# Attention's softmax divisors: turned by VectorE in 32x32 blocks and sent round through DRAM, instead of turned by TensorE

## The chip, the cores and the metric

One core of a Trainium2 chip runs one program. The metric is the time of one execution on the device, in microseconds (us). The kernel before took 1761.09 us (median of 3 runs, 1760.48 to 1762.41).

Engines are named as the profile names them: PE is TensorE (PEld its weight loads), DVE is VectorE, ACT is ScalarE, POOL is GpSimd, SP is SyncE, which here only issues DMAs. Each engine runs its own instructions strictly in the order in which they stand in the program; engines wait for each other through semaphores.

## The reference, cut to what matters

Layer 0 is windowed grouped-query attention with a sink logit per head; layer 1 is a Mamba-2 mixer, which the change does not touch. For every block of 128 queries:

```
s = einsum('bqkgd,bskd->bkgqs', qb, kb).astype(float32) * scale      # 16 heads, 4 KV heads, head dim 64
p = softmax(concatenate([where(mask, s, -inf), sink_col], -1), -1)[..., :-1]
o = einsum('bkgqs,bskd->bqkgd', p, vb)
y_lat = (o * silu(g)) @ w_out
```

The softmax's divisor is one number for each query and head. The kernel does not divide `p`; it multiplies the gate `silu(g)` by the reciprocal of the sum, and then `o` by that. There are 1024 latent queries (8 blocks, each seeing up to 3 latent blocks and 2 context blocks of keys) and 256 context queries (2 blocks that see only the context).

## The kernel before, in words

The program runs, in order: adaLN and the q, k, v, g projections (up to some 250 us), the attention with the other projections woven in (some 250 to 685 us), the tail of the output projection, and layer 1 (from some 700 us). Only the attention has lines that the change touches.

The attention is cut into 40 **units**, one for each block `b` of 128 queries and each KV head `j` with its `R = 4` query heads: first 8 units of the two context blocks (2 key blocks each), then 32 of the latent blocks 0 to 7 (4 or 5 key blocks each). A unit has two halves:

- `att_front`: PE makes the scores `S` (queries on the partitions) for each head; DVE (L781) masks them and takes the row minimum `nm`, ACT (L783) takes the exponential into `sm` and adds up `sums`. POOL adds the sink's term (L786, L788), DVE takes the reciprocal of the 128x4 `sums` (L790).
- `att_back`: for each key block, PE turns the four heads' `sm` (L802) into one of the two `pt` buffers in PSUM, ACT copies it to `ph` (L806), DVE makes the low part `pl` (L807), and PE multiplies both by `v` into `pv` (L808, L809). `pv` has one buffer and holds the head dimension on the partitions and the queries along the row. At the unit's end ACT copies half of `pv` to `co` (L818), DVE adds the halves into `ot` (L821), POOL multiplies by the gate `sgt` (L822), and ACT and POOL split the product for the output projection (L824, L825).

The gate `sgt` also has the head dimension on the partitions, so the 128x4 reciprocals, which have queries on the partitions, must be turned and repeated over each head's 64 partitions. Before the change, POOL widens them to 128x256 (`rs`, L791, one buffer), PE turns the two halves through `pt` (L815, two transposes a unit), and DVE multiplies `sgt` by the result in PSUM (L816).

`att_front` of the next unit is written ahead of `att_back` of this one. What stands in each engine's row is settled by a scheduler when the program is built: each engine gets the ready instructions by priority, and the projections for later (L240 to L242, with their weights loaded by SP at L233, cast by ACT at L223, split by POOL at L225) are put between. `issue_after(x)` adds an ordering edge behind `x`, without a semaphore, to instructions of `x`'s own engine.

Of the kernel before, what the change touches and what calls it, by code (L numbers as in the profile page):

```python
# [9 lines left out]
F32 = mybir.dt.float32  # L10
# [7 lines left out]
P = 128  # L18
# [11 lines left out]
HD = 64  # L30
# [3 lines left out]
R = 4  # L34
# [8 lines left out]
    pj=1, S=2, pt=2, pv=1,  # L43
    rope_b=2, qf=3, qh=3, ql=2, kHH=2, kLL=2, qs=2, sgt=2, sm=8, mx=2, nm=2, es=2, sums=2, ph=2, pl=2, co=1, ot=2,
    oraw=3, h1=3, h1k=8, wada=6, gq=1, sqa=1,
    cacc=2, cctx=1, bT=2, cT=2, xn4=4, xn2=1, bn4=4, bn2=1, sz=2, xw=2, hf=2, hx=2, M=2, bw=2, y2=1, xs=1, uT=2, pj2=2, psX=3, sk=2, dg=2,
)
G0 = 4
AHEAD = 1
# [65 lines left out]
class Kernel:  # L115
# [13 lines left out]
    def t(self, pool, shape, dt, tag, bufs=None):  # L129
        self.n += 1  # L130
        kw = {"bufs": bufs or BUFS.get(tag, 1)}
        return pool.tile(shape, dt, tag=tag, name=f"{tag}_{self.n}", **kw)
# [616 lines left out]
    def att_front(self, p, x, i, j, b):  # L749
        nc, t = self.nc, self.t  # L750
        ps = self.psA
        o = b * P - TT[i][0]
        sg = t(self.psm, [P, 2, P], F32, "sgt")
        nm = t(p, [P, R], F32, "nm")
        sums = t(p, [P, R], F32, "sums")
        qs = t(p, [P, R, P], F32R, "qs")
        nc.gpsimd.dma_start(qs, self.q_d[j][i][:, :, :, o : o + P].rearrange("e s d n -> (s d) e n"))
        nc.sync.dma_start(sg, self.sg_d[j][i][:, :, o : o + P].rearrange("e p n -> p e n"))

        z = j % 2  # L760
        qz = self.qz[z]
        nc.gpsimd.dma_start(qz[z * HD : (z + 1) * HD], self.q_d[j][i][:, z, :, o : o + P].rearrange("e d n -> d e n"))
        if b < 8:
            k0, k1 = max(b - 1, 0), min(b + 2, 8)
        else:
            k0, k1 = 8, 8
        kb = list(range(k0, k1)) + [8, 9]
        c0_ = 512 - (k1 - k0) * P
        m0 = {0: 128, 7: 640}.get(b, 0 if b < 8 else 384)
        W = len(kb) * P  # L770
        sms = []
        for r in range(R):
            S = t(self.psS, [P, 1024], F32, "S")
            for x, (qq, kk) in enumerate(((qs[:, r, :], self.kHH[j]), (qz[:, r, :], self.kL[j // 2]))):
                if k1 > k0:
                    nc.tensor.matmul(S[:, c0_:512], qq, kk[:, k0 * P : k1 * P], start=x == 0, stop=x == 1)  # L776
                scored = nc.tensor.matmul(S[:, 512:768], qq, kk[:, LAT : LAT + CTX], start=x == 0, stop=x == 1)  # L777
            self.scored.append(scored.ins)
            Sv = S[:, c0_:768]
            sm = t(self.psm, [P, 640], F32, "sm")  # L780
            nc.vector.tensor_tensor_reduce(out=sm[:, :W], in0=Sv, in1=self.mask[:, m0 : m0 + W], scale=-SCALE, scalar=self.nsink[:, 4 * j + r : 4 * j + r + 1],  # L781
                                           op0=ALU.add, op1=ALU.min, accum_out=nm[:, r : r + 1])
            nc.scalar.activation(sm[:, :W], sm[:, :W], AF.Exp, bias=nm[:, r : r + 1], scale=-1.0, accum_out=sums[:, r : r + 1])  # L783
            sms.append(sm)
        es = t(p, [P, R], F32, "es")
        nc.gpsimd.tensor_tensor(es, nm, self.sink[:, 4 * j : 4 * j + 4], op=ALU.add)  # L786
        nc.scalar.activation(es, es, AF.Exp)
        nc.gpsimd.tensor_tensor(sums, sums, es, op=ALU.add)  # L788
        rs = t(self.pb, [P, 2, 2, HD], F32, "rs")
        nc.vector.reciprocal(sums, sums)  # L790
        nc.gpsimd.tensor_copy(rs, sums.rearrange("p (x e) -> p e x", e=2).unsqueeze(3).broadcast_to([P, 2, 2, HD]))  # L791
        return j, b, i, o, kb, sms, sg, rs

    def att_back(self, p, st, oH, oL, tick):
        nc, t = self.nc, self.t
        ps = self.psA
        j, b, i, o, kb, sms, sg, rs = st
        pv = t(ps, [P, 512], F32, "pv")
        for x, bb in enumerate(kb):
            pt = t(ps, [P, R, P], F32, "pt")  # L800
            for r in range(R):
                nc.tensor.transpose(pt[:, r, :], sms[r][:, x * P : (x + 1) * P], self.ident)  # L802
            ph = t(self.pb, [P, R * P], F32R, "ph")
            pl = t(self.pb, [P, R * P], F32R, "pl")
            ptf = pt.rearrange("p r n -> p (r n)")
            nc.scalar.copy(ph, ptf)  # L806
            nc.vector.tensor_sub(pl, ptf, ph)  # L807
            nc.tensor.matmul(pv, self.v[:, bb, j, :], ph, start=x == 0, stop=False)  # L808
            mm = nc.tensor.matmul(pv, self.v[:, bb, j, :], pl, start=False, stop=x == len(kb) - 1)  # L809
            self.last.append(mm.ins)  # L810
            tick()

        pt = t(ps, [P, 512], F32, "pt")
        for e in range(2):
            nc.tensor.transpose(pt[:, e * P : (e + 1) * P], rs[:, e].rearrange("p x d -> p (x d)"), self.ident)  # L815
        nc.vector.tensor_mul(sg, sg, pt[:, : 2 * P].rearrange("p (a n) -> p a n", a=2))  # L816
        co = t(self.pb, [HD, 512], F32, "co")
        nc.scalar.copy(co, pv[HD:, :])  # L818
        ot = t(self.pb, [P, 2, P], F32, "ot")
        for e in range(2):  # L820
            nc.vector.tensor_add(ot[e * HD : (e + 1) * HD].rearrange("p a n -> p (a n)"), pv[:HD, e * 256 : (e + 1) * 256], co[:, e * 256 : (e + 1) * 256])  # L821
        nc.gpsimd.tensor_tensor(ot, ot, sg, op=ALU.mult)  # L822
        oh = oH[i][:, 2 * j : 2 * j + 2, o : o + P]
        nc.scalar.copy(oh, ot)  # L824
        nc.gpsimd.tensor_tensor(oL[i][:, 2 * j : 2 * j + 2, o : o + P], ot, oh, op=ALU.subtract)  # L825

    def attention(self, c0, ckv):
        nc, t, a = self.nc, self.t, self.a
        ps = self.psA
# [4 lines left out]
        p = self.pool("att", ctx=c0)  # L834
# [3 lines left out]
        self.load_rope(pq, 512, 512)  # L838
        oH, oL = [None] * 3, [None] * 3
        self.qz = [t(p, [P, R, P], F32R, f"qz{z}") for z in range(2)]  # L840
        for z in range(2):
            nc.gpsimd.memset(self.qz[z][(1 - z) * HD : (2 - z) * HD].bitcast(F32), 0.0)

# [102 lines left out]
        for x, (i, j, b) in enumerate(units):  # L946
            if oH[i] is None:
# [6 lines left out]
                n = TT[i][1]  # L954
# [12 lines left out]
        with ExitStack() as c1:  # L967
# [6 lines left out]
            for i, lo in ((2, 256), (0, 0)):  # L974
                n = TT[i][1] // 2
# [889 lines left out]
```

## Time and profile before

| | |
|---|---|
| runs | 1761.09 us median (1760.48 to 1762.41, 3 runs) |
| profiled execution | 1762.06 us, of which the profiled span is 1760.4 us |
| granted TensorE clock | 0.997 |
| busy, share of the span | PE 98%, PEld 85%, DVE 68%, ACT 50%, POOL 44% |
| the chain that ended last | PE 89%, DVE 4%, ACT 2%, DMA 2%, issue 2% |

The span goes from the first to the last instruction. Busy time of PE counts matmuls that overlap in its pipeline, so 98% does not say that nothing could be squeezed; the chain of work that ended last says which engine set the pace. Idle time of an engine off that chain costs nothing by itself.

### The profile page before, as it was taken

How to read it: one execution, taken by the hardware profiler on the slowest of the kernel's cores; microseconds unless marked ns; L12 is line 12 of the kernel's file. 1: busy time of each engine (PE TensorE's matmuls, PEld its weight loads, DVE VectorE, ACT ScalarE, POOL GpSimd, SP SyncE). 2: the span in 40 equal slices, each digit the busy share in tenths (PEclk: the TensorE clock that was granted, in tenths of full speed). 3: DMA queues.
4: the chain of work that ended last, by engine and by line, in shares of the span. 5: the costliest groups of instructions: out<-in, count | busy, mean ns of one | idle time of the engine just before them, and what ended most of it. 6: DMA issues, size and time to landing. Idle time of an engine off the chain costs nothing.

```text
span 1760.4 us, 28922 instructions
## 1 busy us (share of the span) xinstructions
PE 1732.0 (98%) x10277; PEld 1498.0 (85%) x10277; DVE 1197.1 (68%) x2131; ACT 873.3 (50%) x1905; POOL 771.8 (44%) x1048
## 2 busy tenths in 40 slices
PE   9999999999999999999999999999999999999997
PEld 6897878888888787889898998989889898988886
DVE  5744436788877777585767867677686767776734
ACT  4522247777777775462544534344444444544522
POOL 3331046555565541004454544636455363554311
PEclk9999999999999999999999999999999999999999
DMA  9468866444564436222233332332333333655533
GB/s 362 172 197 259 288 178 144 102 114 96 115 163 129 120 101 226 69 70 66 79 83 90 75 91 69 88 78 76 90 82 80 85 82 78 181 168 172 176 96 132
DMA packets 211389, 225.53 MB, mean 128 GB/s; under 512 B 15788, under 2 KB 149036, under 8 KB 211244
## 3 DMA queue, kind: packets, MB, share of 16 engines
q1 hardware_dynamic: 177180, 205.02, 39.0%
q0 software_dynamic: 34064, 18.65, 5.9%
q8 instruction: 81, 1.33, 0.3%
q14 instruction: 64, 0.52, 0.1%
HBM read 188.78 MB, written 35.13 MB: 127 GB/s over the span
## 4 chain that ended last, share of the span: by engine, by line
PE 89%; DVE 4%; ACT 2%; DMA 2%; issue 2%; POOL 0%; SPq 0%; DVEq 0%; ACTq 0%; POOLq 0%
PE pj L1243 20%; PE pj L1277 10%; PE pj L1682 7%; PE pj L240 7%; PE pj L241 6%; PE pj L242 6%; PE psD L1227 4%; PE pt L802 3%; PE psX L1430 3%; PE psD L1346 2%; PE pv L809 2%; PE pv L808 2%; PE S L776 2%; PE S L777 2%; PE psX L1399 2%
## 5 line engine op out<-in xcount | busy, mean ns | idle before, releaser
L240 PE MATMUL pj<-uH,wh 128*128 128x512 f32 (+1 forms) x632 | 234.0, 370 | 4.2 <-ACT uH L824 1.5
L242 PE MATMUL pj<-uH,wl 128*128 128x512 f32 (+1 forms) x632 | 222.2, 352 | 0.0
L241 PE MATMUL pj<-uL,wh 128*128 128x512 f32 (+1 forms) x632 | 222.1, 351 | 0.0
L1321 POOL TENSOR_TENSOR xw<-xn,dtdec 128x256 f32<-128x256 f32 x144 | 96.0, 668 | 212.6 <-PE psD L1346 72.3
L1243 PE MATMUL pj<-uH,wh 128*128 128x512 f32 x512 | 173.2, 410 | 0.0
L1243 PE MATMUL pj<-uH,wl 128*128 128x512 f32 x512 | 170.3, 403 | 0.0
L1243 PE MATMUL pj<-uL,wh 128*128 128x512 f32 x512 | 168.7, 403 | 0.0
L1277 PE MATMUL pj<-wl,uH 128*128 128x256 f32 x512 | 150.8, 295 | 0.0
L1277 PE MATMUL pj<-wh,uH 128*128 128x256 f32 x512 | 150.3, 293 | 0.0
L1277 PE MATMUL pj<-wh,uL 128*128 128x256 f32 x512 | 149.8, 293 | 0.0
L807 DVE TENSOR_TENSOR pl<-pt,ph 128x512 fp32r<-128x512 f32 x168 | 115.0, 688 | 46.0 <-ACT ph L806 44.8
L240 PEld LDWEIGHTS pj<-uH,wh 128*128 128x128 f32 x632 | 119.6, 189 | 22.9 <-issue 3.6
L242 PEld LDWEIGHTS pj<-uH,wl 128*128 128x128 f32 x632 | 119.4, 189 | 18.4 <-DVE wl L225 1.3
L781 DVE CUSTOM_DVE_ANT_0 sm<-S,mask,nsink 128x640 f32<-128x640 f32 (+2 forms) x160 | 118.9, 773 | 23.8 <-PE S L777 18.2
L1462 ACT ACTIVATE uT<-psX,nw 128x128 f32<-128x128 f32 x128 | 46.6, 364 | 170.9 <-PE psX L1461 169.9
L225 POOL TENSOR_TENSOR wl<-wr,wh 128x512 fp32r<-128x512 f32 x74 | 97.2, 1317 | 77.5 <-ACT wh L223 74.0
L241 PEld LDWEIGHTS pj<-uL,wh 128*128 128x128 f32 x632 | 120.0, 190 | 12.0 <-issue 0.8
L783 ACT ACTIVATE sm<-sm,nm 128x640 f32<-128x640 f32 (+2 forms) x160 | 118.6, 743 | 21.2 <-DVE nm L781 20.6
L806 ACT CAST ph<-pt 128x512 fp32r<-128x512 f32 x168 | 97.9, 585 | 50.5 <-PE pt L802 47.6
L223 ACT CAST wh<-wr 128x512 fp32r<-128x512 f32 (+1 forms) x116 | 74.7, 648 | 83.4 <-PE pj L241 60.3
L1243 PEld LDWEIGHTS pj<-uH,wl 128*128 128x128 f32 x512 | 95.8, 188 | 19.9
L1243 PEld LDWEIGHTS pj<-uL,wh 128*128 128x128 f32 x512 | 95.3, 188 | 19.2
(357 smaller groups left out, 4913.0 us busy)
## 6 DMA issues: line engine op xcount, KB each, us to landing
wr<-w_x SPq DMA_DIRECT2D x32, 512.0 KB, 4.4
M<-acs SPq DMA_DIRECT2D x64, 256.0 KB, 5.1
bw<-acs SPq DMA_DIRECT2D x64, 256.0 KB, 5.4
wr<-w_sk SPq DMA_DIRECT2D x24, 512.0 KB, 4.5
wr<-wg SPq DMA_DIRECT2D x40, 256.0 KB, 4.8
qs<-q POOLq DMA_DIRECT2D x40, 256.0 KB, 4.0
wada<-w_ada SPq DMA_DIRECT2D x16, 512.0 KB, 8.3
wr<-wq SPq DMA_DIRECT2D x32, 256.0 KB, 3.2
```

The lines of the kernel that those rows point to most:

```text
L225: (eng or nc.vector).tensor_tensor(l, raw, h, op=ALU.subtract)
L240: self.nc.tensor.matmul(ps, lh, rh, start=first and i == 0, stop=False)
L241: self.nc.tensor.matmul(ps, lh, rl, start=False, stop=False)
L242: self.last_mm = self.nc.tensor.matmul(ps, ll, rh, start=False, stop=last and i == n - 1)
L781: nc.vector.tensor_tensor_reduce(out=sm[:, :W], in0=Sv, in1=self.mask[:, m0 : m0 + W], scale=-SCALE, scalar=self.nsink[:, 4 * j + r : 4 * ...
L783: nc.scalar.activation(sm[:, :W], sm[:, :W], AF.Exp, bias=nm[:, r : r + 1], scale=-1.0, accum_out=sums[:, r : r + 1])
L806: nc.scalar.copy(ph, ptf)
L807: nc.vector.tensor_sub(pl, ptf, ph)
L1243: self.pe = nc.tensor.matmul(raw[:, 512 * i : 512 * i + 512], l[:, k, :], r[i][:, k, :], start=k + y == 0, stop=k == KT - 1 and y == 2)
L1277: self.pe = nc.tensor.matmul(pj[:, c], l, r[:, k, :], start=c % 2 + q + k + y == 0, stop=c % 2 == 1 and q == 1 and k == 3 and y == 2)
L1321: nc.gpsimd.tensor_tensor(xw, X(st, c).rearrange("p (r h) -> p r h", r=R), self.dtdec[:, c, hd(d, g)].unsqueeze(2).broadcast_to([P, R, HP] ...
L1682: self.pe = nc.tensor.matmul(banks[x], l[:, z, sl], r, start=k == 2 * qs[0] and y == 0, stop=k == 2 * qs[-1] + 1 and y == 2)
```

## The change

The widening copy on POOL, the two transposes on PE and the multiplication out of PSUM go. In their place DVE takes the reciprocals in the first 4 columns of a 128x32 buffer (`s32`, two of them, zeroed once at the start) and turns that buffer in four 32x32 blocks into `sT`. SP stores it to DRAM as 32 short rows of 128 numbers (rows 0 to 3 are the four heads), and two DMAs of SP load it back, each spreading two heads' rows over 64 partitions (`rb`, tag `rs`, two buffers). DVE then multiplies `sgt` by `rb`, both in SBUF.

```diff
-        sums = t(p, [P, R], F32, "sums")
+        s32 = self.s32.pop(0)
+        self.s32.append(s32)
+        sums = s32[:, :R]
...
-        rs = t(self.pb, [P, 2, 2, HD], F32, "rs")
         nc.vector.reciprocal(sums, sums)
-        nc.gpsimd.tensor_copy(rs, sums.rearrange("p (x e) -> p e x", e=2).unsqueeze(3).broadcast_to([P, 2, 2, HD]))
+        turned = t(p, [P, 32], F32, "sT", 2)
+        nc.vector.transpose(turned, s32)
+        rs = t(self.dr, [32, P], F32, f"rs{j}_{b}")
+        nc.sync.dma_start(rs.rearrange("r (b n) -> b r n", b=4), turned)
...
         pv = t(ps, [P, 512], F32, "pv")
+        rb = t(self.pb, [P, 2, P], F32, "rs")
+        def spread():
+            for x in range(2):
+                nc.sync.dma_start(rb[x * HD : (x + 1) * HD], rs[2 * x : 2 * x + 2].unsqueeze(0).broadcast_to([HD, 2, P]))
+        if len(kb) < 4:
+            spread()
...
+            if x == 1 and len(kb) >= 4:
+                with self.tc.issue_after(mm.ins):
+                    spread()
...
-        pt = t(ps, [P, 512], F32, "pt")
-        for e in range(2):
-            nc.tensor.transpose(pt[:, e * P : (e + 1) * P], rs[:, e].rearrange("p x d -> p (x d)"), self.ident)
-        nc.vector.tensor_mul(sg, sg, pt[:, : 2 * P].rearrange("p (a n) -> p a n", a=2))
+        nc.vector.tensor_mul(sg, sg, rb)
```

The change moves the schedule of the whole attention. Three lines of the kernel get new numbers: the multiplication of the gate L816 becomes L828, the sum into `ot` L821 becomes L833, and the low part L807 becomes L819; the mask line L781 becomes L783; the store is L795, the loads back L807.

Two places show what moved. The first is DVE, in the latent blocks 0 to 3. Before, this piece holds the end of a unit: the gate's product (`sgt_1053`) stands seven instructions ahead of the same unit's `ot` (`ot_1129`), and the unit's reciprocal stands 28 rows ahead of the product.

```order
L781 ISA nm_1131_4832 128x1
L807 TENSOR_TENSOR pl_1126_4811<-pt_1124_4805,ph_1125_4810 128x512
L816 TENSOR_TENSOR sgt_1053_4540<-sgt_1053_4540,pt_1127_4819 128x256
L630 TENSOR_TENSOR qf_1151_4906<-pj_1114_4756,cos_488_2569 128x512
L631 STREAM_SHUFFLE rope_b_1154_4909<-pj_1114_4756 128x512
L781 ISA sm_1139_4859,nm_1131_4832<-S_1138_4854,mask_187_661,nsink_188_662 128x640
L781 ISA nm_1131_4832 128x1
L781 ISA sm_1141_4867,nm_1131_4832<-S_1140_4862,mask_187_661,nsink_188_662 128x640
L781 ISA nm_1131_4832 128x1
L821 TENSOR_TENSOR ot_1129_4825<-pv_1104_4732,co_1128_4823 64x256 x2
```

Now the same engine at about the same place, from the turning of a unit's divisors (`sT_1023`) to the product that uses them (`sgt_1011`, with the loaded `rs_1070`):

```order
L793 STREAM_TRANSPOSE sT_1023_4444<-s32_0_492_2575 128x32
L819 TENSOR_TENSOR pl_1042_4517<-pt_1040_4511,ph_1041_4516 128x512
L633 TENSOR_TENSOR qf_1036_4497<-qf_1036_4497,rope_b_1039_4500 128x512
L783 ISA sm_1059_4572,nm_1056_4562<-S_1058_4567,mask_187_661,nsink_188_662 128x640
L783 ISA nm_1056_4562 128x1
L783 ISA sm_1061_4580,nm_1056_4562<-S_1060_4575,mask_187_661,nsink_188_662 128x640
L783 ISA nm_1056_4562 128x1
L819 TENSOR_TENSOR pl_1052_4544<-pt_1050_4538,ph_1051_4543 128x512
L652 TENSOR_TENSOR ql_1037_4498<-qf_1036_4497,qh_1038_4499 128x512
L828 TENSOR_TENSOR sgt_1011_4401<-sgt_1011_4401,rs_1070_4609 128x256
```

The product moved forward by about a unit: it follows the turning after 9 rows instead of the reciprocal after 28, and its own unit's `ot` (`ot_1091`) comes only 26 rows behind it, after the `ot` of the unit ahead.

The second place is SP's row of DMA issues at the same point of the program, before (weights `wr`, queries `q0`, gates `sgt`):

```order
L233 DMA wr_1043_4504<-wq 128x512
L758 DMA sgt_1009_4381<-sg0_0_50_150 128x2x128
L233 DMA wr_1108_4744<-wq 128x512
L663 DMA q0_1_39_139<-qh_1035_4475 64x512 x2
L664 DMA q0_1_39_139<-ql_1034_4474 64x512 x2
L233 DMA wr_1111_4750<-wq 128x512
L758 DMA sgt_1053_4540<-sg1_0_53_153 128x2x128
```

and now:

```order
L233 DMA wr_1111_4768<-wq 128x512
L795 DMA rs0_2_1024_4446<-sT_1023_4444 4x32x32
L807 DMA rs_1070_4609<-rs0_2_1024_4446 64x256 x2
L663 DMA q0_1_39_139<-qh_1038_4499 64x512 x2
L664 DMA q0_1_39_139<-ql_1037_4498 64x512 x2
L233 DMA wr_1114_4774<-wq 128x512
L760 DMA sgt_1055_4561<-sg1_0_53_153 128x2x128
```

The store and the two loads of a unit stand one right behind the other here, so SP stands at the first load until the store has landed, with queries, weights and gates queued behind; the loads do not stand later in the unit, since the edge of `issue_after` is put on PE's instructions only.

More of the change, by code (lines that the diff above doesn't have):

```diff
@@ L45 @@
     oraw=3, h1=3, h1k=8, wada=6, gq=1, sqa=1,
-    cacc=2, cctx=1, bT=2, cT=2, xn4=4, xn2=1, bn4=4, bn2=1, sz=2, xw=2, hf=2, hx=2, M=2, bw=2, y2=1, xs=1, uT=2, pj2=2, psX=3, sk=2, dg=2,
+    cacc=2, cctx=1, bT=2, cT=2, xn4=4, xn2=1, bn4=4, bn2=1, sz=2, xw=2, hf=2, hx=2, M=2, bw=2, y2=1, xs=1, uT=2, pj2=2, psX=3, sk=2, dg=2, rs=2,
 )
@@ L840, in attention @@
         self.qz = [t(p, [P, R, P], F32R, f"qz{z}") for z in range(2)]
+        self.s32 = [t(p, [P, 32], F32, f"s32_{z}") for z in range(2)]
+        for z in range(2):
+            nc.vector.memset(self.s32[z], 0.0)
         for z in range(2):
```

## The prediction

> **What bounds the kernel now.** I read the page's busy shares and chain first, then a table by stage, then who waits for whom in the attention, then the rows of the removed lines.
>
> ```profile
> PE 1732.0 (98%) x10277; PEld 1498.0 (85%) x10277; DVE 1197.1 (68%) x2131; ACT 873.3 (50%) x1905; POOL 771.8 (44%) x1048
> ...
> PE 89%; DVE 4%; ACT 2%; DMA 2%; issue 2%; POOL 0%; SPq 0%; DVEq 0%; ACTq 0%; POOLq 0%
> ```
>
> PE sets the pace over the whole span. The change lies between some 250 and 685 us; the table by stage has, for each stretch, its length and then the busy time of each engine:
>
> ```profile
> core 0: us, PE busy (x) PEld busy (x) DVE busy (x) ACT busy (x) POOL busy (x), PEclk, DMA share, GB/s
> 250.00:310.00 60.00, 58.81 (x338) 49.47 (x337) 41.30 (x127) 45.79 (x129) 42.90 (x71) 1.00 0.63 145
> 310.00:490.00 180.00, 176.74 (x1028) 150.61 (x1027) 145.51 (x312) 131.43 (x291) 100.11 (x145) 1.00 0.47 107
> 490.00:550.00 60.00, 58.61 (x417) 53.98 (x415) 43.24 (x93) 45.93 (x101) 42.66 (x60) 1.00 0.63 163
> 550.00:690.00 140.00, 134.62 (x735) 109.92 (x735) 103.95 (x209) 93.14 (x203) 62.59 (x88) 1.00 0.50 142
> ```
>
> In these 440 us PE is busy 428.8 (97%) and DVE 334.0 (76%), 81% in the stretch from 310 to 490. So PE work taken out shortens the attention, as long as DVE, the next fullest and bound to PE by every `pl` and every `S`, keeps up. How tightly they are bound is in the waits from 250 to 690 us (total, times, longest):
>
> ```profile
> POOL rs L791 <- PE pt L815: 33.0, 20, 3.2
> ...
> PEld pv L809 <- DVE pl L807: 12.1, 27, 1.0
> ...
> DVE sgt L816 <- PE pt L815: 3.6, 4, 1.3
> ```
>
> and, of SP's queue alone:
>
> ```profile
> SPq L233 <- POOL wl L225: 47.6, 26, 6.5
> SPq L233 <- POOL rs L791: 33.0, 9, 6.1
> ```
>
> Of 168 uses of `pl`, PE stood before 27 (16%), 0.45 us each; the other 141 times DVE was early. DVE idles 106 us in this window (440 less 334), mostly for ACT and PE, so a late DVE can partly catch up. PE's own list for the window has nine rows, 10.6 us in all, from
>
> ```profile
> PE pv L809 <- DVE pl L807: 4.0, 13, 0.7
> ...
> PE S L776 <- DVE nm L781: 0.2, 1, 0.2
> ```
>
> and names DVE or ACT as the releaser in each, never a weight or a DMA.
>
> **Removed from PE.** Two transposes a unit, 40 units.
>
> ```profile
> L815 PE MATMUL pt<-ident,rs 128*128 128x128 f32 x80 | 15.3, 272 | 0.0
> ...
> 412.63 0.39 PE L809 MATMUL pv<-pl,v 128*128 128x512 f32 x1
> 412.86 0.38 PE L815 MATMUL pt<-ident,rs 128*128 128x128 f32 x2
> 412.99 0.48 PE L240 MATMUL pj<-uH,wh 128*128 128x512 f32 x1
> 413.31 0.40 PE L241 MATMUL pj<-uL,wh 128*128 128x512 f32 x1
> 413.55 0.39 PE L242 MATMUL pj<-uH,wl 128*128 128x512 f32 x1
> ```
>
> The mean of 272 ns counts what overlaps with the neighbours. What a pair really takes is read from starts: a 512-wide matmul follows another after 0.23 to 0.24 us (413.31 to 413.55; 412.63 to 412.86). From the pair's start to L241 pass 0.45 us, of which L240's own share is 0.23, so the pair takes 0.22 us. 40 x 0.22 = **-8.8 us**, all of it on the engine that sets the pace.
>
> **Removed at the tail.** The last unit's pair stood late in PE's row:
>
> ```profile
> 677.37 0.85 DVE L821 TENSOR_TENSOR ot<-pv,co 64x256 f32<-64x256 f32 x2 [2.77 <-ACT co L818]
> ...
> 680.48 0.42 DVE L816 TENSOR_TENSOR sgt<-sgt,pt 128x256 f32<-128x256 f32 x1
> ...
> 680.98 0.74 POOL L822 TENSOR_TENSOR ot<-ot,sgt 128x256 f32<-128x256 f32 x1 [3.26 <-DVE sgt L816]
> ...
> 683.36 0.50 PE L240 MATMUL pj<-uH,wh 128*128 128x512 f32 x1 [1.53 <-ACT uH L824]
> ```
>
> `ot` was summed at 678.2, but the gate's product followed only at 680.9, then POOL, ACT, and PE, which had idled 1.53 us. With the product done ahead of `ot`, POOL can start 2.7 us earlier and that idle time goes: **-1.5 us**. The bounds are 0 (another input becomes late) and -1.5.
>
> **Removed from POOL.** 40 copies and the 33.0 us that POOL stood before them. No engine's wait on POOL is on PE's way here, so I count it at 0; its cover is that PE sets the pace. It does free the weights' split and SP's weight loads behind it, which pays for SP's new standing (below).
>
> **Added to DVE.** A block turning per unit, and the product now reads two SBUF operands.
>
> ```profile
> L790 DVE RECIPROCAL sums<-sums 128x4 f32<-128x4 f32 x40 | 6.8, 170 | 1.2 <-POOL sums L788 1.0
> ...
> L816 DVE TENSOR_TENSOR sgt<-sgt,pt 128x256 f32<-128x256 f32 x40 | 16.5, 413 | 3.8 <-PE pt L815 3.6
> ...
> L1441 DVE TENSOR_TENSOR y<-y,psX 128x256 f32<-128x256 f32 x64 | 26.5, 414 | 33.2 <-POOL y L1423 16.4 <-PE psX L1430 14.4 <-POOL bw L1374 2.4
> ...
> L1442 DVE TENSOR_TENSOR y<-y,sz 128x256 f32<-128x256 f32 x64 | 38.9, 608 | 1.1
> ```
>
> No block turning is in the trace. A 128x32 operation lies between 128x4 (170 ns) and 128x256 (413 ns); 32 columns are nearer to 4, so 0.17 us, 40 x 0.17 = 6.8 us (up to 16.5). The product has near twins in layer 1: with one operand in PSUM 414 ns, with both in SBUF 608 ns. So 0.41 becomes 0.61 us, 40 x 0.2 = 7.8 us (0 to 7.8). The GPSIMD Engine Reference of the Trainium skill, in its specifications, says that GpSimd shares its SBUF interfaces with VectorE and that they contend when a VectorE instruction has two SBUF inputs; that speaks against the change. The trace agrees by the 608 against the 414 ns; if the rule did not hold here, the product would cost DVE nothing more.
>
> **Added: a round trip through DRAM, and a wait in DVE's row.** The new order (above) puts the product L828 right where the loads should just have landed, a unit ahead of its need. An early wait there holds everything behind it on DVE: the next `pl`, which PE's L809 and the `pt` buffers wait for, and the next mask L783, which frees `S`. The nearest rows for the trip:
>
> ```profile
> sgt<-sg SPq DMA_DIRECT2D x38, 128.0 KB, 2.4
> ...
> sg<-qf SPq DMA_DIRECT2D x8, 256.0 KB, 2.2
> ...
> L758 SPq DMA_DIRECT2D sgt<-sg x40: 359/377/489, 242.0 to 656.5; - x40
> ...
> DMA to landing us min/median/max: 2.1/2.4/4.1
> ```
>
> A store lands after 2.2 us, SP issues a load in 0.38, the second load lands after 2.4: 2.2 + 0.38 + 2.4 = 5.0 us from the store's issue to `rb`. Against it stands DVE's own work between turning and product in the piece shown:
>
> ```profile
> L807 DVE TENSOR_TENSOR pl<-pt,ph 128x512 fp32r<-128x512 f32 x168 | 115.0, 688 | 46.0 <-ACT ph L806 44.8
> ...
> L781 DVE CUSTOM_DVE_ANT_0 sm<-S,mask,nsink 128x640 f32<-128x640 f32 x96 | 81.8, 879 | 11.1 <-PE S L777 7.3 <-PE pt L802 3.3
> ...
> L633 DVE TENSOR_TENSOR qf<-qf,rope_b 128x512 f32<-128x512 f32 x8 | 7.1, 888 | 0.5 <-POOL rope_b L632 0.5
> ...
> L652 DVE TENSOR_TENSOR ql<-qf,qh 128x512 fp32r<-128x512 f32 x8 | 5.6, 700 | 0.8 <-ACT qh L651 0.6
> ```
>
> Two `pl` (1.4), two masks (1.8), 0.9 and 0.7: 4.8 us, and 5.9 at the 81% at which DVE runs there. So `rb` is in time here by 0.9 us, and late by 0.2 if DVE runs without a pause. Other units have less between the two; in the first eight, whose units are short, I expect waits of up to some 2 us. The nearest rows for such waits are other loads from DRAM of what the kernel itself stored a little ahead:
>
> ```profile
> L301 DVE SCALAR_TENSOR_TENSOR h<-h,mod,ut 128x256 f32<-128x256 f32 x8 | 4.0, 494 | 5.6 <-DMA h<-h 5.2 <-issue 0.4
> ...
> L1640 ACT CAST uH<-oraw 128x512 fp32r<-128x512 f32 x32 | 18.9, 619 | 10.2 <-DMA oraw<-uN 9.3 <-PE pj L1277 0.5
> ```
>
> 5.2/8 = 0.65 and 9.3/32 = 0.29 us each. I take 0.35, nearer to the larger group: 40 x 0.35 = 14 us of DVE standing (0 to 76: by the longest landing, 4.1 instead of 2.4 us, each product would stand 1.9). The DMA page of the Trainium skill (DMA: Bandwidth & Descriptors, Anatomy of one DMA) gives some 2.0 us of fixed time per DMA, mostly the receipt of the write. By it the trip would be 4.4 us, an estimate, and the standing nearly nothing; the trace's shortest landing of 2.1 and median of 2.4 us lie above the page.
>
> DVE is thus later by 14 + 6.8 + 7.8 - 3.6 (the wait for the pair, gone) = 25 us over the attention. Of that PE pays a share: at least the 16% of `pl` that have no slack now, at most all. DVE keeps a quarter of its time idle and most `pl` come early, so I take 0.2: **+5 us** (0 to 25).
>
> **SP.** One store and two loads more a unit, 3 x 0.38 = 1.1 us of issue, and 2.2 us of standing until the store has landed. Behind it stand the weights' loads, the gates and the queries' stores. PE waits for no weights in the list above; SP itself stood 47.6 us for POOL's splits and 33.0 us for its copies at the weights' loads, and the copies are gone. I count 0; the bound above is 40 x 2.2 us, if every one met PE.
>
> **Sum.** -8.8 - 1.5 + 5 = -5.3 us on the profiled execution: 1762.06 - 5.3 = 1756.8. That execution stood 0.97 us over the median of the runs, so I forecast a median of **1756.0 us**.
>
> **The rivals.**
>
> *DVE's lateness eats the gain* (no change). If the waits are nearer to the 0.65 us of the first group (26 us) and the turning costs 0.4, DVE is 46 us later and a fifth of it is 9 us: the sum is -1, 1760 us. For it: DVE is 81% full in the longest stretch, and PE stands before 27 `pl` already. Against it: the larger group of such loads waits only 0.29.
>
> *The product's wait becomes the pace* (slower). If the small store with its 128-byte pieces, or the loads behind it, land at the 4.1 us end, the trip takes 6.7 us against DVE's 4.8 to 5.9: a product stands 0.8 to 1.9 us, 1.4 in the mean, 56 us over 40 units. Then the lateness recurs in every unit, `pt` and `S` stay full, and I let PE pay half: 28 us, with 2 for the turning and the dearer product, less 10.3: +20, 1781 us. It decides from about 0.9 us a unit, at a third paid (12 + 2 against 10.3 + 3.5). For it: the product stands a unit before its need, and DVE can't pass it. Against it: a landing of 2.4 in the median.
>
> *The transposes were hidden* (no change, 1761). Against it: 97% busy, and the pair moves the next matmul by 0.22 us in the rows above.
>
> **How the numbers follow.** 0.2%, or 3.5 us, is about what a measurement of this kernel can tell from no change: faster is below 1757.6, slower above 1764.6. The forecast has 0.50, from the full -10.3 (1751) to 1757.6; its own range is 1751 to 1758. DVE eating the gain has 0.24, the hidden transposes 0.04: together 0.28 for no change. The product's wait as the pace has 0.22. The range reaches from 1751 (nothing given back) to 1768, into the slow case, of which I count some half beyond; that leaves some 0.07 below and 0.11 above.
>
> **What would show it.** In the profile after, no L815 and 80 matmuls less on PE; PE's busy time in the attention some 9 us less. DVE's product L828 with a mean near 0.6 us and idle time before it, released by the DMA `rs`: some 14 us in all is right, over 50 us is the slow case. The turning near 0.17 us. POOL without its 33 us. SP standing before L807 for the store, some 2 us a unit. I would be wrong if PE's idle time for `pl` and `S` grew by over 10 us, or if weights appeared among its waits.

## The result, and the profile after

The changed kernel takes **1794.12 us** (median of 6 runs, 1786.93 to 1797.8) against 1761.37 us for the one before, beside it on the same chip: ratio 1.0184, 95% interval [1.0173, 1.0194]. It is 33 us slower; 5 us faster had been forecast. The profiled execution took 1796.62 us, its span is 1794.7 us. Of the kernel with the late product, below, one execution of ten took 2421.41 us at a granted clock of 0.654, and its median is that of the other nine.

The page's busy shares and the chain that ended last, to set beside those of before:

```profile
PE 1739.7 (97%) x10197; PEld 1499.1 (84%) x10197; DVE 1209.9 (67%) x2173; ACT 873.9 (49%) x1905; POOL 756.0 (42%) x1008
...
PE 79%; DMA 9%; DVE 6%; issue 2%; ACT 2%; SPq 1%; POOL 0%; DVEq 0%; ACTq 0%; POOLq 0%
```

The 80 transposes are gone (10277 to 10197 instructions), and still PE's share of the chain falls from 89 to 79%, DMA's rises from 2 to 9%: the trip through DRAM now lies on the way to the end. The table by stage (length, then busy time of PE, PEld, DVE, ACT, POOL, then the granted clock):

```profile
250.00:310.00 60.00, 52.73 (x267) 42.20 (x265) 34.71 (x110) 38.98 (x110) 34.62 (x52) 0.94 0.56 135
310.00:490.00 180.00, 164.68 (x891) 137.61 (x891) 137.63 (x303) 118.08 (x263) 83.46 (x118) 0.95 0.48 112
490.00:550.00 60.00, 55.05 (x356) 47.61 (x355) 46.46 (x98) 41.66 (x92) 36.48 (x46) 1.00 0.58 145
550.00:690.00 140.00, 131.34 (x768) 111.11 (x767) 105.53 (x234) 100.34 (x224) 71.62 (x95) 0.99 0.49 129
```

In these 440 us PE is busy 403.8 instead of 428.8, and where before the clock stood at 1.00 it is now 0.94 and 0.95 in the first two stretches. Who waits for whom from 250 to 690 us, DVE, then PE, then SP's queue:

```profile
DVE sgt L828 <- DMA rs<-rs: 45.6, 28, 3.9
```

```profile
PE pv L821 <- DVE pl L819: 8.6, 8, 3.9
PE S L778 <- DVE nm L783: 7.5, 5, 3.3
PE pj L240 <- DVE rope_b L631: 3.9, 3, 3.2
PE pj L240 <- DVE h L882: 3.1, 3, 1.7
PE pj L240 <- DVE qf L671: 2.9, 1, 2.9
```

```profile
SPq L807 <- DMA rs<-sT: 45.8, 38, 2.8
```

The product of gate and divisors stands 45.6 us for its loads (46.7 with the last units). PE, whose longest wait for `pl` was 0.7 us, now stands up to 3.9 us at a time, and the five longest rows, shown, are all for DVE. SP stands 45.8 us for the stores. The new instructions themselves, by line (busy time, mean ns of one, idle time before them):

```profile
L828 DVE TENSOR_TENSOR sgt<-sgt,rs 128x256 f32<-128x256 f32 x40 | 25.5, 637 | 48.5 <-DMA rs<-rs 46.7 <-issue 1.7
...
L793 DVE STREAM_TRANSPOSE sT<-s 128x32 f32<-128x32 f32 x40 | 8.3, 206 | 0.6
```

One such wait in order of time, DVE, SP and PE in turn (start, duration, engine, line; in brackets the idle time and what ended it). It is the tenth unit, whose turning ended at 330.53:

```profile
336.89 0.43 DVE L828 TENSOR_TENSOR sgt<-sgt,rs 128x256 f32<-128x256 f32 x1 [2.97 <-DMA rs<-rs]
337.23 0.68 DVE L671 SCALAR_TENSOR_TENSOR qf<-qf,pj 128x512 f32<-128x512 f32 x1
337.83 0.68 DVE L819 TENSOR_TENSOR pl<-pt,ph 128x512 fp32r<-128x512 f32 x1
```

```profile
330.55 0.56 SPq L795 DMA_DIRECT2D rs<-sT  x1
332.54 1.13 SPq L807 DMA_DIRECT2D rs<-rs  x2
```

```profile
333.22 0.40 PE L820 MATMUL pv<-ph,v 128*128 128x512 f32 x1
333.46 0.39 PE L821 MATMUL pv<-pl,v 128*128 128x512 f32 x1
...
334.62 0.40 PE L820 MATMUL pv<-ph,v 128*128 128x512 f32 x1
337.96 0.79 PE L240 MATMUL pj<-uH,wh 128*128 128x512 f32 x1 [2.94 <-DVE qf L671]
338.56 0.63 PE L241 MATMUL pj<-uL,wh 128*128 128x512 f32 x1
338.98 0.63 PE L242 MATMUL pj<-uH,wl 128*128 128x512 f32 x1
339.41 0.63 PE L240 MATMUL pj<-uH,wh 128*128 128x512 f32 x1
```

The trip took 336.89 - 330.55 = 6.3 us, and for the last 2.97 of it DVE did nothing. Behind the product in DVE's row stood `qf` and `pl`; PE ran out of work 2.94 us. The first to read the product is GpSimd's multiplication behind this unit's own `ot`, and that `ot` starts only at 346.55. Then the matmuls follow each other at 0.42 to 0.43 us (338.56, 338.98, 339.41) where ahead of the gap it was 0.24 (333.22, 333.46): the second price of the gap is the clock. The table in pieces of 10 us shows it:

```profile
270.00:280.00 10.00, 6.49 (x21) 5.47 (x22) 5.78 (x17) 4.44 (x14) 3.09 (x6) 0.66 0.39 107
310.00:320.00 10.00, 6.67 (x30) 5.59 (x30) 5.38 (x15) 4.24 (x12) 3.42 (x7) 0.83 0.59 140
340.00:350.00 10.00, 10.00 (x50) 8.54 (x49) 5.30 (x13) 5.62 (x15) 4.07 (x8) 0.80 0.46 97
440.00:450.00 10.00, 9.47 (x39) 8.29 (x40) 7.05 (x15) 4.46 (x10) 3.26 (x6) 0.68 0.24 53
```

PE is busy there and does less (the last row has 39 matmuls in 9.47 us). Over all such pieces from 250 to 720 us, busy time by (1 - clock) comes to some 13 us.

### The profile page after: what moved, and what is told of

The parts are those of the page before. It is cut to its first block, busy times and chain, and to the rows that moved or that the text cites. A ratio compares the mean times of both kernels' runs of the same rounds, so it can differ in the third digit from the quotient of the medians.

```text
span 1794.7 us, 28878 instructions
## 1 busy us (share of the span) xinstructions
PE 1739.7 (97%) x10197; PEld 1499.1 (84%) x10197; DVE 1209.9 (67%) x2173; ACT 873.9 (49%) x1905; POOL 756.0 (42%) x1008
## 4 chain that ended last, share of the span: by engine, by line
PE 79%; DMA 9%; DVE 6%; issue 2%; ACT 2%; SPq 1%; POOL 0%; DVEq 0%; ACTq 0%; POOLq 0%
PE pj L1258 19%; PE pj L1292 10%; PE pj L1697 7%; PE pj L240 5%; PE pj L241 5%; PE pj L242 5%; DMA rs<-rs 4%; PE psD L1242 4%; PE psX L1445 3%; DMA rs<-sT 3%; PE psD L1361 2%; PE psX L1414 2%; PE psX L1413 2%; PE psX L1420 1%; PE pt L814 1%
## 5 line engine op out<-in xcount | busy, mean ns | idle before, releaser
L225 POOL TENSOR_TENSOR wl<-wr,wh 128x512 fp32r<-128x512 f32 x74 | 97.0, 1313 | 103.7 <-ACT wh L223 102.5
L819 DVE TENSOR_TENSOR pl<-pt,ph 128x512 fp32r<-128x512 f32 x168 | 113.9, 685 | 29.9 <-ACT ph L818 28.1
L783 DVE CUSTOM_DVE_ANT_0 sm<-S,mask,nsink 128x640 f32<-128x640 f32 (+2 forms) x160 | 118.9, 770 | 16.2 <-PE S L779 12.5
```

What stands on the lines that cost most here:

```text
L225: (eng or nc.vector).tensor_tensor(l, raw, h, op=ALU.subtract)
```

## The experiments

Three theories. **Theory 1**: VectorE stands in its row for data that nobody needs yet; low parts, masks and drains of projections queue behind, and TensorE runs dry. **Theory 2**: SyncE stands some 46 us for the stores, and gates, weights and queries behind it are late. **Theory 3**: the scheduler's other order as such. The kernel before took 1760.6 to 1761.4 us in each group; ratios are to it. Kernels that multiply the gate by ones leave out the division by the softmax's sums.

### The product late in the row

The product goes behind the unit's last low part; nothing else changes.

```diff
-            nc.vector.tensor_sub(pl, ptf, ph)
+            low = nc.vector.tensor_sub(pl, ptf, ph)
...
-        nc.vector.tensor_mul(sg, sg, rb)
+        with self.tc.issue_after(low.ins):
+            nc.vector.tensor_mul(sg, sg, rb)
```

> The changed kernel, but the gate's product is put behind the unit's last low part in VectorE's row, so that it stands where it stood before the change, a unit later than now. Theory 1 (VectorE stands in its row for data that nobody needs yet, and TensorE runs dry and loses clock): the standing for the loaded divisors falls from 46.7 us to under 5, the granted clock returns to 0.997, and the time is the old one less the transposes and the tail's wait, plus 1 to 2 us for the dearer product: 1751 to 1755 us. Theory 2 (SyncE stands 46.8 us for the stores to land, and weights, gates and queries behind it come late): its row is the same, so the time stays at 1785 us or more. Theory 3 (the scheduler's other order as such): 1775 to 1795.

Measured: 1765.69 us, ratio 1.0023 [1.0011, 1.0034]. Its product's row by line, and DVE's wait from 250 to 330 us:

```profile
L829 DVE TENSOR_TENSOR sgt<-sgt,rs 128x256 f32<-128x256 f32 x40 | 21.0, 525 | 14.4 <-DMA rs<-rs 13.6 <-DMA sgt<-sg 0.8
```

```profile
DVE sgt L829 <- DMA rs<-rs: 13.4, 6, 3.8
```

One ordering edge returns 28 of the 33 us and takes the wait from 46.7 to 13.6 us; Theories 2 and 3, at 1775 us and more, are off by 9 us or more. Theory 1's full gain (1751 to 1755) was missed, though: 13.4 of the 13.6 us lie ahead of 330 us, where the short context units run.

### The trip made, but not read

The store and both loads stay; the product reads a tile of ones.

```diff
-        nc.vector.tensor_mul(sg, sg, rb)
+        nc.vector.tensor_mul(sg, sg, self.flat)
```

> The changed kernel with store and loads as they are, but the gate is multiplied by a constant tile of ones in SBUF: the output lacks the division. Theory 1: no wait on VectorE, 1750 to 1755 us. Theory 2: SyncE still stands some 47 us for the stores, so 1785 us or more. Theory 3: 1775 to 1795, since the order is of the new kind.

Measured: 1761.72 us, ratio 1.0013 [1.0001, 1.0024]. The product's row of its groups by line:

```profile
L828 DVE TENSOR_TENSOR sgt<-sgt,flat 128x256 f32<-128x256 f32 x40 | 24.4, 609 | 26.7 <-DMA sgt<-sg 26.0 <-POOL s L790 0.4
```

Above Theory 1's forecast and below those of the other two. SP's standing is still there (46.4 us against 46.8 in the changed kernel) and 32 us are gone, so most of the loss is the read. But an early product with nothing to wait for in `rs` still waits 26 us, for the gate's own load.

### Nothing turned at all

The kernel before without the copy on GpSimd and the two transposes; the product reads ones. What is removed, alone.

```diff
-        nc.gpsimd.tensor_copy(rs, sums.rearrange("p (x e) -> p e x", e=2)...)
...
-        for e in range(2):
-            nc.tensor.transpose(pt[:, e * P : (e + 1) * P], rs[:, e]...)
-        nc.vector.tensor_mul(sg, sg, pt[:, : 2 * P]...)
+        nc.vector.tensor_mul(sg, sg, self.flat)
```

> The kernel before without the widening copy on GpSimd and without the two transposes a unit; the gate is multiplied by a constant tile of ones, so the output lacks the division. It bounds what the removal can bring. If TensorE sets the pace: 8.8 us for the transposes and 1.5 for the tail, so 1751 us, to within 2. If the transposes were hidden: 1761.

Measured: 1751.47 us, ratio 0.9944 [0.993, 0.9959]. The gain the forecast began from is there: 9.6 us less, for 8.8 + 1.5 forecast. The product's row:

```profile
L812 DVE TENSOR_TENSOR sgt<-sgt,flat 128x256 f32<-128x256 f32 x40 | 26.5, 663 | 25.5 <-DMA sgt<-sg 22.1 <-POOL sums L788 3.1
```

So this kernel has the dearer product too, and 25.5 us of standing ahead of it (the longest 3.1 us), and still gains 9.6 of the 10.3 us forecast. A total of standing is not a price.

### The trip added to the kernel before

The path of before stays whole; turning, store and loads are added, and VectorE reads one column of the loaded tile ahead of its product.

```diff
+        turned = t(p, [P, 32], F32, "sT", 2)
+        nc.vector.transpose(turned, s32)
+        nc.sync.dma_start(rd.rearrange("r (b n) -> b r n", b=4), turned)
...
+        spread()
...
+        nc.vector.tensor_copy(seen, rb[:, 0, 0:1])
```

> The kernel before, whole, with the old transposes and the old product, and beside them the block turning, the store, the two loads and a 128x1 copy on VectorE that reads what was loaded (its result is not used). Theory 1 (the standing is the cost): VectorE stands for the copy as it did for the product, less where the copy lies further behind the store; at 20 to 45 us of standing and 0.7 us paid for each, 1775 to 1795 us. Theory 2 (SyncE): 1785 or more, whatever the copy waits. Theory 3 (it was the new order or the removal, not the trip): 1761 to 1765.

Measured: 1793.08 us, ratio 1.019 [1.0171, 1.0209]. The reading copy, by line:

```profile
L828 DVE COPY seen<-rb 128x1 f32<-128x1 f32 x40 | 6.1, 153 | 41.2 <-DMA rb<-rs 40.9
```

With the old transposes kept, the turning, the trip and a copy of 128 numbers that waits for it cost 32 us, about what the whole change loses in the net. Neither the dearer product nor the removal of the old path is needed for the loss, which speaks against Theory 3 (1761 to 1765); Theories 1 and 2 had both allowed this time.

### By stage: context units alone, latent units early, latent units late

Three kernels keep the path of before in some units. *Context only* has the changed path where `b >= 8`; *latent early* has it where `b < 8`; *mixed* has it where `b < 8`, with the product behind the last low part. The edit of mixed:

```diff
-        turned = t(p, [P, 32], F32, "sT", 2)
+        if b < 8:
+            turned = t(p, [P, 32], F32, "sT", 2)
...
+        else:
+            rs = t(self.pb, [P, 2, 2, HD], F32, "rw", 1)
+            nc.gpsimd.tensor_copy(rs, sums.rearrange(...)...)
...
+        if new:
+            with self.tc.issue_after(low.ins):
+                nc.vector.tensor_mul(sg, sg, rb)
+        else:
+            pt = t(ps, [P, 512], F32, "pt")
+            for e in range(2):
+                nc.tensor.transpose(pt[:, e * P : (e + 1) * P], rs[:, e]...)
+            nc.vector.tensor_mul(sg, sg, pt[:, : 2 * P]...)
```

> The other half: the changed path as it was written, early product, in the 8 context units alone, the path of before in the 32 latent units. Theory 1: the late product gave back 28 of the 33 us, and it could help the latent units only, so the context units' part is what was left: 1766.4 less the 1760 that a waitless version would have, some 6 us, less 0.2 x 8.8 = 1.8 saved: 1763 to 1768, with the clock falling at most near 270 to 310 us. If the first gap in the context units carries the later ones with it (the clock stays low, the queues never catch up), the time is far above: 1775 and more.

> The 8 context units on the path of before, the 32 latent units on the changed path with the product where the change left it (early). Together with the kernel that changes the context units alone (1775.1, +14.3) it says whether the loss adds up by stage. Theory 1: the latent units' early product costs 28 us against the late one (1794.1 less 1766.4), so 1751 + some 15 to 28 = 1766 to 1779, with product waits of some 25 to 35 us, nearly all in 310 to 690 us. If the context units' gaps were what put the latent units out of step, it is near the mixed kernel: 1751 to 1756.

> The 8 context units keep the path of before (POOL's copy, TensorE's two transposes, the product out of PSUM); the 32 latent units take the changed path with the product behind the unit's last low part. Theory 1 (a product that stands in VectorE's row ahead of its data is the loss): the 13.6 us of product waits left in the kernel with the late product lay in the context units and are gone; 32 of 40 units keep the gain, 0.8 x 8.8 = 7.0, and 1.5 at the tail, against 0.8 of the 10 us that the kernel with the unread trip had above the one that turns nothing: 1758 to 1762 us, product wait under 3 us. Theory 2 (SyncE's standing for the stores is the loss): it stands for 32 units still, some 38 us: no better than the late product in all units, 1764 to 1768.

Measured: context only 1775.09 us, ratio 1.0077 [1.0061, 1.0093]; latent early 1783.02, 1.0116 [1.01, 1.0132]; **mixed 1751.07 us, 0.994 [0.9927, 0.9953]**. The two halves add up: +14.3 and +22.1 are 36.4, the change has +32.8. All three lie outside Theory 1's ranges: the 8 context units cost more than the 6 us expected (1775 and more had been the sign that their gaps carry over into the later units, but then the two halves would not add up), latent early is 4 us over its range, and mixed 7 us under. The product's row of latent early, then of mixed:

```profile
L834 DVE TENSOR_TENSOR sgt<-sgt,rs 128x256 f32<-128x256 f32 x32 | 19.3, 603 | 33.1 <-DMA rs<-rs 27.2 <-issue 5.6
```

```profile
L835 DVE TENSOR_TENSOR sgt<-sgt,rs 128x256 f32<-128x256 f32 x32 | 16.9, 528 | 0.0
```

And mixed by stage:

```profile
250.00:310.00 60.00, 58.72 (x338) 49.53 (x337) 41.41 (x128) 45.80 (x129) 42.80 (x72) 1.00 0.64 144
310.00:490.00 180.00, 177.50 (x1030) 151.57 (x1029) 154.66 (x341) 135.76 (x301) 98.07 (x133) 1.00 0.54 128
```

With the product late, none of the 32 waits at all, the clock is 1.00, and the round trip through DRAM costs nothing that can be seen. That one edge, with the order that the scheduler makes of it, is worth 32 us in these 32 units. Mixed beats both kernels.

### SyncE's standing, and the turning, each by itself

*Mixed with the trip carried* is mixed with the turning, the store and the loads added in the context units, unread. *Carry only* is the kernel with the unread trip, less the turning (the store takes the unturned buffer). *Turn only* is the kernel that turns nothing, with the turnings added and no DMA behind them.

The edit of mixed with the trip carried, in the branch of the context units:

```diff
+            turned = t(p, [P, 32], F32, "sT", 2)
+            nc.vector.transpose(turned, s32)
+            nc.sync.dma_start(self.rd.rearrange("r (b n) -> b r n", b=4), turned)
```

Of carry only, against the kernel with the unread trip:

```diff
-        nc.vector.transpose(turned, s32)
...
-        nc.sync.dma_start(rs.rearrange("r (b n) -> b r n", b=4), turned)
+        nc.sync.dma_start(rs.rearrange("r (b n) -> b r n", b=4), s32)
```

Of turn only, against the kernel that turns nothing:

```diff
+        nc.vector.transpose(turned, s32)
```

> The mixed kernel (1751.1), and in the 8 context units the turning, the store and the two loads added beside the path of before, read by nobody. Theory 2 (SyncE standing for the context units' stores, with gates and queries queued behind it, is what those units lose): 1758 to 1763, and VectorE waits for the gates over 5 us more in 250 to 320 us. Theory 1 (the read, early or late, of a trip too long for a short unit): 1751 to 1754, with SyncE standing 10 to 16 us more and nobody behind it late.

> As the kernel whose product multiplies by constant ones, and the turning left out too: the store takes the unturned 128x32 buffer behind the reciprocal, the two loads land in a tile that nobody reads. Leaves out the division. What stays above the kernel that turns nothing (1751.5) is SyncE's standing and the three DMAs. Theory 1 (VectorE's time counts): the turning's 8.3 us of VectorE were most of the 10 us left with the unread trip: 1752 to 1756. Theory 2 (SyncE standing some 46 us): 1758 to 1762, all of it.

> As the kernel that turns nothing, and VectorE's 40 turnings of the 128x32 buffer added (8.3 us), with no DMA behind them. Leaves out the division. Theory 1: 1755 to 1760 (TensorE pays half or more of VectorE's 8.3 us). Theory 2: 1751 to 1753, since SyncE stands for nothing here.

Measured: mixed with the trip carried 1751.99 us, 0.9945 [0.9932, 0.9957]; carry only 1763.76, 1.0016 [1.0007, 1.0025]; turn only 1755.94, 0.9966 [0.9954, 0.9978]. The longest entry for SP's queue in mixed with the trip carried, from 250 to 720 us:

```profile
SPq L816 <- DMA rs<-sT: 52.7, 36, 3.8
```

SP stands 52.7 us for stores, more than in the changed kernel, and the time is that of mixed: Theory 2 falls as the cause of the 33 us. Carry only is the one result on its side: 12 us over the kernel that turns nothing, and so above Theory 2's 1758 to 1762 as well as Theory 1's 1752 to 1756. There the product stands early for its gate:

```profile
L826 DVE TENSOR_TENSOR sgt<-sgt,flat 128x256 f32<-128x256 f32 x40 | 22.7, 568 | 29.5 <-DMA sgt<-sg 28.2 <-POOL uL L835 1.1
```

The kernel that turns nothing waits 22.1 us for its gates at that place, and is 12 us faster. I read carry only as the same fault by another load, with gates later behind SP's stores; 6 us more of waiting do not account for 12, and no run takes it apart. Turn only is 4.5 us over the kernel that turns nothing, from another group of runs: PE pays about half of the 8.3 us there. In mixed, 32 turnings show no cost.

### What TensorE pays for VectorE's time

The kernel before, with work added on VectorE behind the reciprocals and nothing else: 3 products of 128x256 in each unit (*small pieces*), 15 products of 128x2048 (*pieces of 2.4 us*), 8 of 128x4096 (*pieces of 4.6 us*); the edit of the last.

```diff
-        nc.vector.reciprocal(sums, sums)
+        rec = nc.vector.reciprocal(sums, sums)
+        self.unit = getattr(self, "unit", 0) + 1
+        if self.unit % 5 == 3:
+            with self.tc.issue_after(rec.ins):
+                nc.vector.tensor_mul(self.idle, self.one.broadcast_to([P, 4096]), self.one.broadcast_to([P, 4096]))
```

> The kernel before, and three more products of 128x256 in SBUF on VectorE behind each unit's reciprocal, 120 in all of some 0.41 us: about 49 us of VectorE, in pieces of one product that the scheduler puts between others. It measures the share of VectorE's time that TensorE pays in this stage when it comes in small pieces. The prediction's share of 0.2 gives 1761 + 10 = 1771; a share of 0.7, as the changed kernel's waits look, gives 1795.

> The kernel before, and 15 products of 128x2048 in SBUF on VectorE, each in one piece of some 3.3 us behind the reciprocal of units 2, 5 and 7 of every 8: about the same 49 us of VectorE, in pieces as long as the longest waits of the changed kernel. If only VectorE's total counts, it is the time of the kernel with the small pieces within 5 us. If TensorE's buffers cover small pieces and not long ones (Theory 1: TensorE runs dry and its granted clock falls behind the gap), it is 15 us or more above that one, with gaps of TensorE over 1.5 us and a granted clock of 0.6 to 0.9 behind them.

> The kernel before, and 8 instructions of 128x4096 on VectorE behind the reciprocal of every fifth unit. At the rate of the 128x2048 pieces (2.26 to 2.84 us each, 36.5 us together) some 4.3 to 4.9 us each, 35 to 39 us together: the same total in fewer, longer pieces. If TensorE pays a fixed share (0.48 of it, as with the pieces of 2.4 us): 1778 to 1780, granted clock 0.997. If what counts is how long one stretch is (buffers cover about the first 1.3 us, and a TensorE gap of over 2 us is followed by some 5 us at 0.6 to 0.8 of the clock): 8 x (3.2 + 1.3) = 36 us: 1792 to 1800, granted clock 0.993 or less.

Their rows by line, in that order:

```profile
L795 DVE TENSOR_TENSOR idle<-idle,flat 128x256 f32<-128x256 f32 x120 | 69.1, 576 | 0.8
```

```profile
L794 DVE TENSOR_TENSOR idle<-idle 128x2048 f32<-128x2048 f32 x15 | 36.5, 2433 | 0.0
```

```profile
L794 DVE TENSOR_TENSOR idle<-one 128x4096 bf16<-128x4096 f32 x8 | 36.4, 4551 | 0.0
```

| on VectorE | added | time, ratio | over before | share paid | mean clock |
|---|---|---|---|---|---|
| 120 of 0.58 us | 69.1 us | 1775.12, 1.0075 [1.0061, 1.0089] | 14.2 | 0.21 | 0.997 |
| 15 of 2.4 us | 36.5 us | 1778.44, 1.0096 [1.0081, 1.0112] | 17.6 | 0.48 | 0.998 |
| 8 of 4.6 us | 36.4 us | 1790.95, 1.0172 [1.0157, 1.0188] | 30.3 | 0.83 | 0.991 |

The price goes with the length of one stretch, not with the total: the last two add the same 36 us, and one costs 18, the other 30. They also differ in number, place and operands, which no run separates. (The small pieces took 576 ns, not the 410 expected. The pieces of 2.4 us, planned for 3.3, missed their forecast of 15 us over the small ones and a clock of 0.6 to 0.9, so longer ones were run; these ended 1 us under theirs, 1792 to 1800.) In the long pieces TensorE has eight gaps of 2.0 to 3.5 us, one behind each piece, 20.5 us together, and the clock falls behind six of them:

```profile
270.00:280.00 10.00, 9.57 (x45) 8.04 (x46) 6.66 (x20) 5.54 (x17) 7.13 (x11) 0.83 0.59 128
350.00:360.00 10.00, 7.97 (x40) 6.75 (x39) 7.90 (x15) 5.24 (x12) 6.24 (x7) 0.83 0.31 65
470.00:480.00 10.00, 7.18 (x25) 6.01 (x26) 7.59 (x11) 2.22 (x5) 3.68 (x2) 0.66 0.25 72
```

Over all eight such pieces of 10 us the clock takes some 9.5 us; 20.5 + 9.5 is the measured 30. So TensorE's cover against a silent VectorE is some 4.6 - 2.6 = 2.0 us, by the mean gap, and in these eight places each microsecond past it cost one and some of the clock. In pieces of 2.4 us no 10 us of the attention have a clock under 1.00. The cover alone is not the whole price: by it the small pieces would be free and those of 2.4 us cost 15 x 0.4 = 6 us, and they cost 14 and 18.

### The product on GpSimd

The changed kernel, with the early product moved to another engine.

```diff
-        nc.vector.tensor_mul(sg, sg, rb)
+        nc.gpsimd.tensor_tensor(sg, sg, rb, op=ALU.mult)
```

> The changed kernel with the product of gate and loaded reciprocals on GpSimd, early as the change has it: GpSimd stands for the trip, not VectorE. Theory 1 (the loss is that low parts and masks stand behind the wait in VectorE's row): TensorE gets its low parts on time, 1752 to 1762, VectorE waiting for rs never. If a wait of that length costs the same on whichever engine it stands (GpSimd's sums and split weights behind it): 1785 to 1800.

Measured: 1762.03 us, ratio 1.0008 [0.9996, 1.002]; the upper end of Theory 1's range. By line:

```profile
L828 POOL TENSOR_TENSOR sgt<-sgt,rs 128x256 f32<-128x256 f32 x40 | 30.8, 770 | 93.8 <-DMA rs<-rs 90.1 <-issue 3.5 <-PE pt L814 0.2
```

Twice the wait, 90.1 us, on an engine that feeds TensorE from further off, costs 32 us less than 46.7 us of it on VectorE. It is still 11 us over mixed, so it is not free.

## Why the prediction was wrong, step by step

- **Removed from PE, -8.8, and the tail, -1.5: right.** The kernel that turns nothing is 9.6 us faster.
- **Removed from POOL, counted 0; SP, counted 0: right within what was measured.** The kernel that turns nothing lacks POOL's copies and gained no more than PE's terms; mixed with the trip carried has SP standing 52.7 us at mixed's time. Only carry only leaves some of SP's effect open.
- **Turning, 0.17 us: 0.206. Product, 0.61 us: 0.637.** Small misses. The product's mean has single ones up to 2.18 us in it; placed late it is 0.525.
- **The trip, 5.0 us: 5.8 in the median** from the turning's end to the product (5.2 to 8.3). SP issues these DMAs in 0.56 us, not 0.38, the store lands after 2.0, and the product starts 2.8 us behind the issue of the second load, where 2.4 had been taken. In 9 units the store itself waited over 0.2 us for SP. By the section of the Trainium skill that the prediction cites (DMA: Bandwidth & Descriptors, Anatomy of one DMA) it would be 4.4 us, but that section has its 2.0 us for DMAs that GpSimd issues, and SP issues these.
- **DVE's own work against it, 4.8 us, 5.9 with its pauses: 3.7 and 4.8 in the median.** I read one piece of the row for all units, and it was a full one: in some 35 of 40 units DVE's work between turning and product was less than 4.8 us. I also chose the end with the pauses, by which the data was in time by 0.9 us. In the mean DVE came to the product 4.9 us behind the turning, pauses and all, and started it after 6.1: **1.2 us of wait a unit (46.7 / 40 for the loads) where I had taken 0.35**, from loads (L1640, L301) that stand elsewhere in their rows. This is the first step that failed; the rival's own range, 0.8 to 1.9 us, held it.
- **The share of DVE's lateness that PE pays, 0.2: the step that made the sign wrong.** By the prediction's own sum DVE is later by 46.7 + 8.3 + 9.0 - 3.6 = 60 us (25 forecast), and PE paid 1794.1 - 1751.5 = 43 us, or 0.7 of it. 0.2 is right for work in small pieces (0.21 measured); it had been read from 27 waits of 0.45 us at `pl`. These waits come in stretches up to 3.9 us, on top of the work, and longer stretches cost 0.48 and 0.83. The mean wait was asked for, its longest was not. Nor is 0.7 a price to carry on: the kernel that turns nothing stands 25.5 us ahead of its product with hardly a loss, and why its waits are so much cheaper is not settled.
- **Not foreseen: the clock.** Behind PE's gaps the granted clock falls, some 13 of the 43 us. PE's listed waits from 250 to 690 us account for most of the rest: 34.8 us in thirteen rows, 10.6 in nine before, 24 more.
- *The product's wait becomes the pace* was the rival that came, by its mechanism and near its wait: 1.4 us a unit (1.2 measured). Its time, 1781 us (1794), fell short, since it let PE pay half, where it is 0.7 with the clock. Its reason was another: it had a DMA land after 4.1 us, but the store landed after 2.0, and the wait came of slower issues, a later second load and DVE's shorter work.
- What was to show it: PE's idle time for `pl` and `S` grew by more than the 10 us named (from 5.0 to 16.6 us in the rows of `pv` for `pl` and of `S` for `nm`), and no weights stand in the thirteen rows. The other sign, over 50 us ahead of the product, was just missed.
- The last subtraction is off by 0.2: 1756.8 less 0.97 is 1755.8, not 1756.0. Nothing hangs on it.

What stays open: no run holds the order of the changed kernel fixed and takes only its waits away (the scheduler orders each kernel anew), so Theory 3 is bounded, by 1761.7 us with the trip unread, and not excluded as a part of the 10 us left there. Nor does a formula for the 43 us come out of the lengths of the waits.

## What to carry to other kernels

An in-order engine that feeds the bottleneck must not carry a wait ahead of its need: put the consumer of a transfer just ahead of its own reader, not where the transfer should just have landed. Look at the longest stretch of such a wait, on top of the engine's other work, against what the bottleneck has buffered (some 2 us in the kernel with pieces of 4.6 us), before multiplying its total by an average share: longer stretches cost a larger share here, by a law that these runs leave open. And compare a trip with the least work that may stand against it in any unit, not with the work of one.

## What the runs showed of the hardware

- After a gap of 2.0 to 3.5 us in TensorE's work, its matmuls of 512 columns followed at 0.42 to 0.43 us instead of 0.23 to 0.24, for some microseconds (six of eight gaps in the kernel with pieces of 4.6 us). TensorE: Matmul & The Clock Gate of the Trainium skill (Part 1) has half the clock after an idle window of about 3.4 us and 426.7 ns for such a matmul; the pace agrees, but here gaps well under 3.4 us were enough, and not every one of them was. The traces suggest why: in each execution the slow stretches of the attention last 3.4 or 6.8 us and start on a grid of 3.41 us. In the kernel with pieces of 4.6 us TensorE was busy 0.81 of the 3.41 us from 304.79, and the clock was 0.50 in the next 3.41; a gap of 2.62 us at 409.43 lay across two such stretches (busy 2.25 and 1.73 us), and the clock stayed at 1.00. In the kernel with the trip added a longest gap of 1.26 us was enough: busy 1.65 of the 3.40 us from 613.20, then a clock of 0.50. That fits, with a few exceptions, a clock which falls when TensorE was idle for more than about half of one stretch; it is a reading of the traces, and no run tests it.
- A store of 16 KB in 32 short rows lands in 2.0 us, much like one of 256 KB (2.2 in the median, kernel before); each small DMA costs SP 0.56 us to issue, against 0.38 for the gate's load of 128 KB.
- A product with both operands in SBUF took 0.42 us or up to 2.18, for the same shape; with an operand in PSUM it was 0.413 in the mean. In the changed kernel the 11 of 40 that took over 0.5 us all ran beside an operation of GpSimd on two tiles, mostly the split of weights (L225); the 16 with no GpSimd operation beside them took 0.42 to 0.43.
